# Decoder block on one core: the softmax factor moved into the transposing matrix, and eight modulation dot products moved from the a_u stage to gate B

## The chip, the core and the metric

The kernel runs on one core of a Trainium2 chip. The metric is device time in microseconds (us) of one execution, median of several. TensorE (PE) multiplies matrices, VectorE (DVE) and ScalarE (ACT) work element by element, GpSimd (POOL) takes some of that work, and SyncE (SP) issues most of the loads from HBM. Each engine executes its own instructions strictly in the order in which the program gives them; semaphores order work between engines.

## What is computed

A conditioned decoder block for 512 positions and 1024 channels. Cut to what the change touches:

```python
mod = silu(c) @ w_ada + b_ada            # shift1, scale1, gate1, shift2, scale2, gate2
h = rms_norm(x, norm1_g) * (1 + scale1) + shift1
a_u, a_v, q, k, v, qi, ki, wi, g_a, g_b = split(h @ w_in)
y_a = chunked_gmlp(gelu(a_u), gelu(a_v), ...)
# y_b: causal attention, 8 heads, over the top-k keys that the indexer selects
p = softmax(att); o = p @ v_sel
merged = sigmoid(g_a) * (y_a @ w_proj_a) + sigmoid(g_b) * (y_b @ w_proj_b)
x = x + gate1 * (merged @ w_out)         # then RMSNorm, modulation, SwiGLU FFN
```

Two details matter. The division of the softmax by its row sum can stand anywhere between the exponential and the product with V. And every entry of `mod` is a dot product of a row of the transposed `w_ada` with silu(c): gate1 (section 2 in the code), shift2 (3) and scale2 (4) take eight dot products of 128 entries each.

## The kernel before

Most products are formed from two halves of a number (`hi`, `lo`), as three matmuls of type fp32r (`mm3`, lines 66 to 68), so that a product of 128x128 weights with 512 columns is three matmuls. The program is written by hand in one order. The stages in question:

- **a_u** (159 to 222 us): `opt_b(W_AU[g], ...)` for four groups of 256 columns; between them DVE works on the gMLP and on the top-k search.
- **gate A and projection A** (222 to 291 us): two rounds of `xround` and four groups of `W_PA`.
- **attention and gate B** (291 to 373 us): 16 units `u` of two heads each, first four units over 512 keys, then four over 384, 256 and 128. The loop over `s` (line 1260) runs four steps of different units side by side: `at_pv(s-3)`, `at_qk(s)` with `at_soft_a(s)`, `at_T(s-2)`, `at_soft_b(s-1)`, the exponential `at_exp(s)`, and after these one or two K tiles of gate B (`gb_part`, list `GBN`; matmuls `pgb`). Gate B's weights are eight chunks, two for each group of `W_GB`.
- **projection B** from 373 us on.

For a unit, `at_soft_a` (L1183) adds the mask and takes row maxima on DVE, `at_exp` (L1193) exponentiates on ACT and gives row sums, `at_soft_b` takes reciprocals (L1200) and scales the two probability tiles on DVE (L1202). `at_T` (L1216) transposes them block by block with PE into PSUM (`pT`), ACT copies that to `th` (L1273), DVE forms the rest `tl` (L1274), and `at_pv` multiplies with V.

**The stream of loads.** `stream` lists the weight chunks ("w") and the modulation rows ("m") in the order of their use; `group(..., nm=, mraw=)` puts `nm` rows behind each chunk, taken from one iterator (`mm_`: sections 2, 3, 4 in this order). `get(i, ahead)` prepares everything up to two chunks ahead: for a chunk ACT makes `hi` (L134) and DVE or POOL `lo` (L138), for a row DVE does the dot product (L209: one custom instruction and one read of the accumulator). A load takes its buffer in the order of the stream. Rows of the a_u stage use the single buffer `acc`, rows of projection A the buffers A2 and A3 (`mraw`), rows of gate B (`mraw=False`) the three `raw` buffers that the weight chunks use too (`RAWB = 3`), so that a load there waits for the third load before it to be used up. SP issues them in order (L107, L115, L205).

Of the kernel before, what the change touches and what calls it, by code (L numbers as in the profile page):

```python
# [9 lines left out]
F32 = mybir.dt.float32  # L10
F32R = mybir.dt.float32r
I32 = mybir.dt.int32
AF = mybir.ActivationFunctionType
OP = mybir.AluOpType
# [14 lines left out]
def block_kernel(ctx: ExitStack, tc: tile.TileContext, x, x_t, c_row, positions, w_ada_t, w_first, w_in, w_blocks,  # L29
# [3 lines left out]
    T, V, A, P, SY = nc.tensor, nc.vector, nc.scalar, nc.gpsimd, nc.sync  # L33
    ctx.enter_context(tc.manual_schedule())
    tiny = ctx.enter_context(tc.tile_pool(name="tiny", bufs=1))
    base = ctx.enter_context(tc.tile_pool(name="base", bufs=1))
# [3 lines left out]
    w_in, w_ffn_in, w_ffn_out = w_in[0], w_ffn_in[0], w_ffn_out[0]  # L40
# [14 lines left out]
    def bank(k, name="bank"):  # L55
        return psum.tile([128, 512], F32, name=name, tag=f"b{k}", bufs=1)

    def f(ap):
        return ap.bitcast(F32)
# [22 lines left out]
    def add_w(src, kts, c0, n, lo=None, where=None):  # L82
        stream.append(dict(kind="w", src=src, kts=kts, c0=c0, n=n, lo=lo or V, where=where))
        wseq.append(len(stream) - 1)
        return len(stream) - 1

    def add_m(dma, fn, early=False, mid=True):
        stream.append(dict(kind="m", fn=fn, dma=dma, early=early, mid=not early and mid))
        return len(stream) - 1
# [76 lines left out]
    def get(i, ahead=2):  # L166
        k = wseq.index(i)
        ensure(wseq[min(k + ahead, len(wseq) - 1)])
        return chunk[i]
# [10 lines left out]
    ident = tiny.tile([128, 128], F32, name="ident")  # L180
# [50 lines left out]
    def group(src, c0, n=256, K=8, mods=None, pool=False, where=None, nm=1, mraw="A2"):  # L231
        ids = []
        for k0 in range(0, K, 4):
            ids.append(add_w(src, list(range(k0, min(K, k0 + 4))), c0, n,
                             P if pool == 2 or pool and k0 % 8 == 0 else V, where.pop(0) if where else None))
            for _ in range(nm if isinstance(nm, int) else nm[k0 // 4]):
                m = next(mods, None) if mods is not None else None
                if m is not None:
                    add_m(*m, mid=mods is mm_ and (mraw[k0 // 4] if isinstance(mraw, tuple) else mraw))
        return ids  # L240
# [12 lines left out]
    def mods_mid():  # L253
        for sec in (2, 3, 4):
            yield from mod_sec(sec)
    mm_ = mods_mid()
    dram = ctx.enter_context(tc.tile_pool(name="dram", bufs=1, space=bass.MemoryType.DRAM))
    W_AV = [[add_w(w_in, [k0, k0 + 1], 1024 + 512 * h, 512, V if k0 % 4 else P) for k0 in range(0, 8, 2)] for h in range(2)]
    W_AU = [group(w_in, 256 * g, pool=2, mods=mm_, mraw="acc") for g in range(4)]
    xsum = {(r, n): dram.tile([128, 1024], F32, name=f"xsum{r}{n}") for r in range(2) for n in (1, 2, 3, 4)}  # L260

    def blk(r, k):
# [15 lines left out]
    for r in range(2):  # L278
# [2 lines left out]
            W_X[r].append(add_w(b, [0, 1, 2, 3], 0, 256, V if p in (2, 5) else P, 48 if p in (1, 4) else 16))  # L281
        for g in (2 * r, 2 * r + 1):
            W_PA.append(group(w_pa, 256 * g, mods=mm_, pool=True, nm=(1 - g % 2,) * 2, mraw=("A2", "A3") if g % 2 == 0 else "A2"))
    W_GB = [group(w_in, 5192 + 256 * g, pool=2 * (g == 1), mods=mm_, nm=1, mraw=False)
            for g in range(4)]
    stream[W_GB[1][0]]["lo"] = V
    W_PB = [group(w_pb, 256 * g, mods=mm_, nm=((0, 1), (1, 1), (1, 0), (0, 0))[g], mraw="k_hi") for g in range(4)]
# [499 lines left out]
    def opt_b(ids, K, rhs, banks, evac, per_chunk=None, post=None, midway=None, step=None, ahead=2, t0=0):  # L787
        pb = [bank(b, "pb") for b in banks]
        for i in ids:
            if per_chunk:  # L790
                per_chunk()
            hi, lo = get(i, ahead)
            kts = stream[i]["kts"]
            for j, kt in enumerate(kts):
                for m in range(2):
                    cc = slice(m * 128, (m + 1) * 128)
                    mm3(pb[m][:, t0:], (hi[:, j, cc], lo[:, j, cc]), tuple(t[:, t0:] for t in rhs[kt]), kt == 0,
                        kt == K - 1)
                if midway and j == 1:
                    midway()  # L800
            if step:
                step()
            if i == W_PB[3][-1]:
                sec_tasks(True)
            if i == ids[-1]:
                evac(pb)
            if post:
                post()
            sec_tasks()
# [8 lines left out]
    def nbanks():  # L818
        GB_[0] ^= 1
        return (0, 1) if GB_[0] else (2, 3)  # L820
# [222 lines left out]
    def au_evac(g):  # L1043
        def ev(pb):
            u = mid.tile([128, 2, S], F32, name="u", tag="A1" if g % 2 else "A0", bufs=1)
            for m in range(2):
                A.activation(u[:, m], pb[m], AF.Gelu_apprx_tanh)
                ub[2 * g + m] = u[:, m]
        return ev

    for g in range(4):
        opt_b(W_AU[g], 8, hT, nbanks(), au_evac(g), au_tasks, au_post)


    aun = [(i, hp) for i in (3, 2, 1, 0) for hp in range(4)]
    AS = {}
# [131 lines left out]
    def at_exp(u):  # L1188
        i, hp = aun[u]
        n = (i + 1) * 128  # L1190
        pt, mx = AS["p", u]
        for e in range(2):
            A.activation(pt[e][:, :n], pt[e][:, :n], AF.Exp, scale=SCALE, bias=mx[:, 2 + e:3 + e],  # L1193
                         accum_out=mx[:, 4 + e:5 + e])

    def at_soft_b(u):
        i, hp = aun[u]
        n = (i + 1) * 128
        pt, mx = AS["p", u]
        V.reciprocal(mx[:, 6:8], mx[:, 4:6])  # L1200
        for e in range(2):
            V.tensor_scalar(pt[e][:, :n], pt[e][:, :n], mx[:, 6 + e:7 + e], None, op0=OP.mult)  # L1202

    def at_T(u):
        i, hp = aun[u]
        pt, _ = AS["p", u]
        th = mid.tile([128, 4, 2, 128], F32R, name="th", tag="A2", bufs=1)
        tl = mid.tile([128, 4, 2, 128], F32R, name="tl", tag="A3", bufs=1)
        AS["t", u] = (th, tl)
        ev = []  # L1210
        for s0 in range(0, i + 1, 2):
            ns = min(2, i + 1 - s0)
            p = bank(4 + s0 // 2, "pT")
            for s in range(ns):
                for e in range(2):
                    T.transpose(p[:, (s * 2 + e) * 128:(s * 2 + e + 1) * 128],  # L1216
                                pt[e][:, (s0 + s) * 128:(s0 + s + 1) * 128], ident)
            o = th[:, s0:s0 + ns].rearrange("p s e n -> p (s e n)")
            ol = tl[:, s0:s0 + ns].rearrange("p s e n -> p (s e n)")
            ev.append((o, ol, p[:, :ns * 256]))  # L1220
        return ev

    def at_pv(u):
        i, hp = aun[u]
        th, tl = AS["t", u]
        g = hp // 2
        p = bank(6, "pv")
        for s in range(i + 1):
            mm3(p[:, :256], (v_hi[:, s, g * 128:(g + 1) * 128], v_lo[:, s, g * 128:(g + 1) * 128]),
                (th[:, s].rearrange("p e n -> p (e n)"), tl[:, s].rearrange("p e n -> p (e n)")),  # L1230
                s == 0, s == i)
        o = slice(i * 128, (i + 1) * 128)
        pp = p[:, :256].rearrange("p (e n) -> p e n", e=2)
        return S2B[hp][:, :, o], S2B[4 + hp][:, :, o], pp

    NU = len(aun)
    gbp = {}

    def gb_part(n, ahead=2):
        for k in range(gbn[0], min(gbn[0] + n, 32)):  # L1240
            g, kt = divmod(k, 8)
            i = W_GB[g][kt // 4]
            hi, lo = get(i, ahead)
# [16 lines left out]
    for s in range(NU + 3):  # L1260
        if s >= 3:
            yh, yl, pp = at_pv(s - 3)
            A.activation(yh, pp, AF.Copy)
            V.tensor_sub(yl, pp, f(yh))
        if s < NU:
            at_qk(s)
            at_soft_a(s)
            if s == 0:
                pa_last[0]()
                at_split(2)  # L1270
        if 2 <= s <= NU + 1:
            for o, ol, p in at_T(s - 2):
                A.activation(o, p, AF.Copy)  # L1273
                V.tensor_sub(ol, p, f(o))  # L1274
        if 1 <= s <= NU:
            at_soft_b(s - 1)
        low = at_split(s + 2, True) if 0 < s < NU - 2 else lambda: None
        if s < NU:
            at_exp(s)
        low()  # L1280
        gb_part(GBN[s], 2 if s else 1)
    mbank[0] = 6
# [503 lines left out]
    for q in range(-2, NQ):  # L1786
        g, u = 2 + q // 2, q % 2
        d = sd[q]
# [210 lines left out]
    for tk in range(2):  # L1999
        for z in range(2) if tk else (None,):  # L2000
# [4 lines left out]
            n = c.stop - c.start  # L2005
# [12 lines left out]
            else:  # L2018
# [3 lines left out]
                                       scale=1.0 / 1024, scalar=ss2[:, tk, 3:4], op0=OP.mult, op1=OP.add,  # L2022
# [62 lines left out]
```

## Time and profile before

| | before |
|---|---|
| median of 3 runs | 791.38 us (791.23 to 862.42) |
| the profiled execution, its own time | 791.98 us |
| its span, first to last instruction | 790.0 us |
| PE busy | 778.3 us (99%) |
| DVE busy | 663.7 us (84%) |
| ACT busy | 443.2 us (56%) |

Busy is the union of an engine's instructions. For PE the end of a matmul is modelled and lies behind the start of the next one, so PE's rate is read from the distance between starts. The chain of waits is followed back from the last instruction; where two engines are equally late, it shows one of them.

### The profile page before, as it was taken

Reading aid. Unit: us, or ns where it says so; the run is one execution under the profiler, and the core shown is the slowest. Engines: PE = TensorE matmul, PEld = TensorE weight load, DVE = VectorE, ACT = ScalarE, POOL = GpSimd, SP = SyncE. Lnnn points to the kernel's source line nnn. Section 1 sums busy time; section 2 is a strip of 40 time slices with the busy share of each in tenths; the row PEclk is TensorE's granted clock in tenths of the full one; section 3 lists DMA queues with packets and bytes.
Section 4 is the critical chain, followed back from the end, with each engine's and each line's share of the span. In section 5 each row is a group of like instructions: output and inputs, shape, how many; then the busy total and the mean of one; then the engine's idle time right before and its main releaser. Section 6 shows DMA issues by size and latency. Waiting matters only on the chain.

```text
span 790.0 us, 12600 instructions
## 1 busy us (share of the span) xinstructions
PE 778.3 (99%) x4747; PEld 694.5 (88%) x4747; DVE 663.7 (84%) x1114; ACT 443.2 (56%) x777; POOL 181.4 (23%) x220
## 2 busy tenths in 40 slices
PE   8999999999999999999999999999999999999996
PEld 6779988878988988988888899999999999878885
DVE  5988887688897799886787879889999888898777
ACT  6556455443362636666536577555665566576654
POOL 2064234574353501000010000313121322100001
PEclk9999999999999999999999999999999999999999
DMA  9959454789763733148692503989998968666664
GB/s 361 416 156 242 119 146 122 217 231 243 212 215 107 235 112 107 54 135 278 232 234 56 187 1 107 255 251 268 258 259 222 260 201 212 177 200 209 209 192 147
DMA packets 89887, 155.05 MB, mean 196 GB/s; under 512 B 7010, under 2 KB 54770, under 8 KB 89635
## 3 DMA queue, kind: packets, MB, share of 16 engines
q1 hardware_dynamic: 72976, 116.05, 44.6%
q0 software_dynamic: 15952, 37.17, 20.9%
q10 hardware_dynamic: 898, 1.04, 0.4%
q8 instruction: 37, 0.61, 0.3%
q14 instruction: 24, 0.19, 0.1%
HBM read 150.16 MB, written 33.56 MB: 233 GB/s over the span
## 4 chain that ended last, share of the span: by engine, by line
PE 64%; DVE 17%; DMA 9%; ACT 5%; issue 4%; POOL 0%; SPq 0%; POOLq 0%; ACTq 0%; DVEq 0%
PE R L66 5%; PE R L68 5%; PE R L67 5%; PE pb L66 5%; PE pb L67 5%; PE pb L68 5%; DMA mraw<-in_w_ada_t_dram 3%; DMA raw<-in_w_ffn_in_dram 3%; DMA raw<-in_w_ffn_out_dram 3%; PE pfo L67 2%; PE pfo L68 2%; PE pfo L66 2%; PE pav L66 2%; PE pav L67 2%; PE pav L68 2%
## 5 line engine op out<-in xcount | busy, mean ns | idle before, releaser
L134 ACT ACTIVATE hi<-raw 128x1024 fp32r<-128x1024 f32 (+1 forms) x111 | 114.5, 1032 | 81.6 <-PE pb L67 32.4
L138 DVE TENSOR_TENSOR lo<-raw,hi 128x1024 fp32r<-128x1024 f32 (+2 forms) x77 | 90.3, 1174 | 26.9 <-ACT hi L134 26.0
L138 POOL TENSOR_TENSOR lo<-raw,hi 128x1024 fp32r<-128x1024 f32 x27 | 69.5, 2577 | 100.2 <-ACT hi L134 69.6
L67 PE MATMUL pfo<-lo,za 128*128 128x512 f32 (+1 forms) x144 | 55.5, 386 | 0.2 <-DVE lo L138 0.2
L66 PE MATMUL pfo<-hi,za 128*128 128x512 f32 (+1 forms) x144 | 55.5, 385 | 0.0
L68 PE MATMUL pfo<-hi,za 128*128 128x512 f32 (+1 forms) x144 | 55.3, 384 | 0.0
L209 DVE CUSTOM_DVE_ANT_0 mraw<-mraw,scb,cols 128x1024 f32<-128x1024 f32 x24 | 37.6, 1568 | 11.7 <-DMA mraw<-in_w_ada_t_dram 11.7
L66 PE MATMUL R<-tb,sx 128*128 128x256 f32 x160 | 45.0, 281 | 0.3 <-ACT gr L462 0.3
L67 PE MATMUL R<-tb,sx 128*128 128x256 f32 x160 | 44.3, 277 | 0.0
L68 PE MATMUL R<-tb,sx 128*128 128x256 f32 x160 | 44.3, 277 | 0.0
L68 PE MATMUL R<-tb,lo 128*128 128x256 f32 x160 | 44.2, 277 | 0.0
L67 PE MATMUL R<-tb,hi 128*128 128x256 f32 x160 | 44.2, 276 | 0.0
L66 PE MATMUL R<-tb,hi 128*128 128x256 f32 x160 | 44.2, 276 | 0.0
L66 PE MATMUL pb<-h,hi 128*128 128x512 f32 (+1 forms) x112 | 42.7, 382 | 0.0
L68 PE MATMUL pb<-h,lo 128*128 128x512 f32 (+1 forms) x112 | 41.9, 374 | 0.0
L67 PE MATMUL pb<-h,hi 128*128 128x512 f32 (+1 forms) x112 | 41.9, 374 | 0.0
L351 POOL COPY sm<-sm 128x1 f32<-128x1 f32 x36 | 23.2, 644 | 78.7 <-ACT sm L350 78.7
L331 POOL DMA_DIRECT2D wsum<-in_w_ffn_out_dram x24 | 21.2, 885 | 78.0 <-DMA wsum<-wsum 46.1
L66 PEld LDWEIGHTS pfo<-hi,za 128*128 128x128 f32 x144 | 27.1, 188 | 6.1 <-ACT ps L1925 0.6
L67 PEld LDWEIGHTS pfo<-lo,za 128*128 128x128 f32 x144 | 27.1, 188 | 6.1 <-DVE lo L138 0.9
L68 PEld LDWEIGHTS pfo<-hi,za 128*128 128x128 f32 x144 | 27.1, 188 | 5.2
L66 PEld LDWEIGHTS R<-tb,sx 128*128 128x128 f32 x160 | 30.1, 188 | 0.9 <-ACT gr L462 0.5
(398 smaller groups left out, 2697.0 us busy)
## 6 DMA issues: line engine op xcount, KB each, us to landing
raw<-in_w_ffn_in_dram SPq DMA_DIRECT2D x44, 512.0 KB, 5.7
raw<-in_w_in_dram SPq DMA_DIRECT2D x30, 512.0 KB, 3.8
wsum<-in_w_ffn_out_dram POOLq DMA_DIRECT2D x30, 512.0 KB, 8.3
mraw<-in_w_ada_t_dram SPq DMA_DIRECT2D x24, 512.0 KB, 6.3
raw<-wsum SPq DMA_DIRECT2D x20, 512.0 KB, 3.8
s<-in_w_ada_t_dram SPq DMA_DIRECT2D x16, 512.0 KB, 8.8
raw<-in_w_ffn_out_dram SPq DMA_DIRECT2D x16, 512.0 KB, 4.6
xsum<-in_w_blocks_dram POOLq DMA_DIRECT2D x12, 512.0 KB, 6.3
```

The lines of the kernel that those rows point to most:

```text
L66: T.matmul(o, wh, rh, start=start, stop=False, **kw)
L67: T.matmul(o, wh, rlo, start=False, stop=False, **kw)
L68: T.matmul(o, wlo, rh, start=False, stop=stop, **kw)
L134: A.activation(hi[:, :m], e["raw"][:, :m], AF.Copy)
L138: e["lo"].tensor_sub(lo[:, :m], e["raw"][:, :m], f(hi[:, :m]))
L209: V.tensor_tensor_reduce(out=raw[:, o], in0=raw[:, o], in1=c, scale=1.0, scalar=col if o.start else bias, op0=OP.mult, op1=OP.add, accum_o ...
L331: P.dma_start(wsum[n][o], src, accum_op=OP.add)
L351: P.tensor_copy(t, t)
```

## The change

`at_soft_b` no longer scales the probabilities. Instead `at_diag`, called one step after the exponential, has ACT write two 128x128 matrices per unit that hold the reciprocal row sums on their diagonal, and `at_T` multiplies by these, with an ordinary fp32 matmul in place of the transpose. The matrices live in one tile `dg` with four places, in a buffer (`hs4`) that gate A leaves free. And the a_u groups take no modulation rows any more, while gate B takes two behind each chunk in place of one; since the iterator is shared, projection A and gate B also work on other rows than before, in the same number there (four) and twice the number here (sixteen).

```diff
-    W_AU = [group(w_in, 256 * g, pool=2, mods=mm_, mraw="acc") for g in range(4)]
+    W_AU = [group(w_in, 256 * g, pool=2) for g in range(4)]
...
-    W_GB = [group(w_in, 5192 + 256 * g, pool=2 * (g == 1), mods=mm_, nm=1, mraw=False)
+    W_GB = [group(w_in, 5192 + 256 * g, pool=2 * (g == 1), mods=mm_, nm=2, mraw=False)
...
         V.reciprocal(mx[:, 6:8], mx[:, 4:6])
+
+    dgs = []
+
+    def at_diag(u):
+        if not dgs:
+            dgs.append(base.tile([128, 4, 2, 128], F32, name="dg", tag="hs4", bufs=1))
+        mx = AS["p", u][1]
+        AS["d", u] = dgs[0][:, u % 4]
         for e in range(2):
-            V.tensor_scalar(pt[e][:, :n], pt[e][:, :n], mx[:, 6 + e:7 + e], None, op0=OP.mult)
+            A.activation(AS["d", u][:, e], ident, AF.Copy, scale=mx[:, 6 + e:7 + e])
...
-                    T.transpose(p[:, (s * 2 + e) * 128:(s * 2 + e + 1) * 128],
-                                pt[e][:, (s0 + s) * 128:(s0 + s + 1) * 128], ident)
+                    T.matmul(p[:, (s * 2 + e) * 128:(s * 2 + e + 1) * 128],
+                             pt[e][:, (s0 + s) * 128:(s0 + s + 1) * 128], AS["d", u][:, e], start=True, stop=True)
...
             at_exp(s)
+        if 1 <= s <= NU:
+            at_diag(s - 1)
         low()
```

On PE, in step 2 of the attention loop (`qk` are the scores of unit 2, `pT` the turned probabilities of unit 0, `pgb` gate B):

```order
 L67 MATMUL qk<-k_lo,qh 128x512
 L68 MATMUL qk<-k_hi,ql 128x512
-L1216 MATMUL pT<-ident,pt 128x128 x8
+L1224 MATMUL pT<-dg,pt 128x128 x8
 L66 MATMUL pgb<-h_155,hi 128x512
 L67 MATMUL pgb<-h_157,hi 128x512
```

The eight instructions stand where they stood; the right-hand operand is `dg`, and so is it in the 15 other units (80 instructions in all).

On DVE, at the end of projection A, just ahead of the first unit's `at_soft_a` (L1183; `raw,GG` and `raw,Gc` are modulation dot products, the rows of 128x1 their accumulator, `lo` is gate B's second chunk):

```order
 L773 TENSOR_SCALAR sco_638<-sco_638 128x256
 L1070 TENSOR_TENSOR ql<-qf_615,qh 128x256
-L209 ISA raw,Gc<-raw,scb,cols 128x1024
-L209 ISA Gc 128x1
+L209 ISA raw,GG_88<-raw,scb,cols 128x1024
+L209 ISA GG_88 128x1
+L209 ISA raw,GG_88<-raw,scb,cols 128x1024
+L209 ISA GG_88 128x1
 L138 TENSOR_TENSOR lo<-raw,hi 128x1024
 L1183 ISA pt,mx<-qk,sco_640 128x512
```

A second dot product stands in front of the chunk's `lo` and the first unit's softmax; likewise at the seven later places where a chunk is prepared.

On SP's queue, the loads of gate B's first chunks (`raw<-in_w_in_dram`) and rows (`raw<-in_w_ada_t_dram`):

```order
 L115 DMA raw<-in_w_in_dram 128x4x256
-L205 DMA raw<-in_w_ada_t_dram 128x1024
+L205 DMA raw<-in_w_ada_t_dram 128x1024 x2
 L115 DMA raw<-in_w_in_dram 128x4x256
-L205 DMA raw<-in_w_ada_t_dram 128x1024
+L205 DMA raw<-in_w_ada_t_dram 128x1024 x2
```

With three buffers, the load of a chunk now takes the buffer of the chunk before it, where it took that of the load ahead of that chunk.

## Rows read from the trace of the kernel before

**Rows 1.** The page's header and its slices of PE and PE's clock.

```profile
span 790.0 us, 12600 instructions
PE   8999999999999999999999999999999999999996
PEclk9999999999999999999999999999999999999999
```

**Rows 2.** Waits (engine, line, waited for: us in total, times, longest), two rows.

```profile
ACT yb L1263 <- PE pv L68: 11.5, 13, 1.7
...
PE zx L1116 <- DVE zx L1126: 0.4, 1, 0.4
```

**Rows 3.** Busy time by stage: a_u, and attention with gate B.

```profile
core 0: us, PE busy (x) PEld busy (x) DVE busy (x) ACT busy (x) POOL busy (x), PEclk, DMA share, GB/s
159.00:222.00 63.00, 63.00 (x366) 54.99 (x365) 53.89 (x94) 28.13 (x37) 32.63 (x20) 1.00 0.79 216
...
291.30:372.90 81.60, 81.49 (x481) 72.08 (x480) 68.23 (x201) 52.04 (x130) 5.59 (x5) 1.00 0.45 145
```

**Rows 4.** Groups of PE by form, 291.3 to 372.9: count, busy us, mean ns, idle before.

```profile
L66 PE MATMUL pgb<-h,hi 128*128 128x512 f32 x64 | 26.5, 414 | 0.0
...
L1216 PE MATMUL pT<-ident,pt 128*128 128x128 f32 x80 | 11.3, 273 | 0.0
...
L1166 PE MATMUL qk<-k_pl,qf 128*128 128x128 f32 x16 | 2.4, 275 | 0.0
```

**Rows 5.** The chain of waits, 308.6 to 372.9, by line.

```profile
by line: PE pgb L66 18.7%; PE pgb L68 18.6%; PE pgb L67 18.5%; PE pT L1216 10.9%; PE pv L67 7.0%; PE pv L68 6.4%; PE pv L66 6.4%; PE qk L68 3.7%; PE qk L67 3.7%; PE qk L66 3.7%; PE qk L1166 2.8%
```

**Rows 6.** The chain of waits, single pieces: start, us to the next piece, what, how many.

```profile
311.16 0.87 PE pT L1216 x8
312.03 0.23 PE pgb L66
...
350.18 0.45 PE qk L1166 x4
350.62 0.44 PE pT L1216 x4
```

**Rows 7.** Groups of DVE, 290 to 375: the scaling and gate B's dot products.

```profile
L1202 DVE TENSOR_SCALAR pt<-pt,mx 128x512 f32<-128x512 f32 (+3 forms) x32 | 10.9, 384 | 0.6
L209 DVE CUSTOM_DVE_ANT_0 raw<-raw,scb,cols 128x1024 f32<-128x1024 f32 x8 | 10.2, 1280 | 0.0
```

**Rows 8.** ACT on 128x128 elements, by form, whole span.

```profile
L1193 ACT ACTIVATE pt<-pt,mx 128x128 f32<-128x128 f32 x8 | 3.2, 395 | 1.8 <-DVE mx L1185 1.8
L424 ACT ACTIVATE sn<-ropes 128x128 f32<-128x128 f32 x1 | 0.3, 296 | 0.0
```

**Rows 9.** SP's issues around gate B's first chunks; last, time to landing of `raw` loads.

```profile
283.82 0.37 SPq L115 DMA_DIRECT2D raw<-in_w_in_dram  x1
288.40 0.34 SPq L205 DMA_DIRECT2D raw<-in_w_ada_t_dram  x1
...
DMA to landing us min/median/max: 3.3/3.8/4.5
```

**Rows 10.** DVE and ACT around the first unit's softmax, in time.

```profile
287.15 1.22 DVE L138 TENSOR_TENSOR lo<-raw,hi 128x1024 fp32r<-128x1024 f32 x1
287.60 1.06 ACT L134 ACTIVATE hi<-raw 128x1024 fp32r<-128x1024 f32 x1 [5.81 <-DMA raw<-in_w_in_dram]
289.09 1.28 DVE L209 CUSTOM_DVE_ANT_0 raw<-raw,scb,cols 128x1024 f32<-128x1024 f32 x1
292.20 0.69 DVE L1183 CUSTOM_DVE_ANT_0 pt<-qk,sco 128x512 f32<-128x512 f32 x1 [0.68 <-PE qk L68]
```

**Rows 11.** The chain of waits, 303 to 309 us: start, us to the next piece, what.

```profile
303.22 0.88 DVE pt L1202 x2
...
307.92 0.60 DVE tl L1274
...
308.56 0.40 PE pv L67
```

## The prediction

> **What bounds the kernel now.** I began with the page's slices. PE's row reads 9 in all but the first and last of its 40 slices, and the row of its granted clock reads 9 in every one [rows 1]. Busy alone proves little, since the ends of matmuls are modelled. So I read the waits next: in the whole span PE waited for DVE just once for as much as 0.4 us, in the a_u stage behind VectorE's `zx` [rows 2]. The busy times by stage say the same of the two stages that the change touches: PE 63.00 of 63.00 us in a_u, 81.49 of 81.60 us in attention with gate B, where DVE has 68.2 and ACT 52.0 us [rows 3]. Last I followed the chain of waits through the attention stage. From 308.6 to 372.9 us every piece of it is a matmul: gate B 55.8%, transposes 10.9%, the rest scores and values [rows 5]. No DVE, ACT or DMA piece occurs. So here an instruction added to PE lengthens the kernel by its whole cost, and one taken from DVE shortens it by nothing. Ahead of that, from 292 to 308 us, the chain runs over DVE: the softmax, the scaling and `tl` follow each other with hardly a gap until `pv` starts at 308.56 [rows 11]. There both engines are full at once.
>
> **The products on PE.** The change turns 80 transposes [rows 4] into 80 fp32 matmuls of the same shape: 4 units times 8, 6, 4 and 2 blocks. What a transpose costs is the distance between starts, not its 273 ns: eight last 0.87 us and four 0.44 us [rows 6], 0.109 us each. The trace has no product with `dg`, but it has its twin two pieces away: the scores of the last four units, plain fp32 matmuls of 128x128 with 128 columns (L1166). The code issues two of them per unit, eight in all, and the trace has 16 records [rows 4], so one matmul is two passes; four records last 0.45 us [rows 6], which makes 0.225 us a matmul. So 80 x (0.225 - 0.109) = 9.3 us, all of it on the path. From below the change could cost nothing here if `dg` ran in one pass as the identity does; nothing in the rows says so, since the operand's type is that of L1166. From above nothing dearer is near: weight loads of this form already lie within the 0.45 us. I take 9.3 us.
>
> A rule of the Trainium skill speaks against the change more strongly. "TensorE: Matmul & The Clock Gate" (section Terms) says that the transpose mode is four times faster for FP32, and "FP8 and Floating Point Precision" (section TensorE Precision Notes) that true FP32 takes four passes through the array. By the first rule a product would cost three more transposes than a transpose does, 80 x 3 x 0.109 = 26 us. The measured ratio of the twin to the transpose is 0.225 / 0.109 = 2.1, not four, and that is what I go by.
>
> **VectorE.** Removed are 32 scalings, 10.9 us [rows 7]. Added to the stage are eight dot products; the eight that stand there take 1.280 us each, 10.2 us in all [rows 7]. So DVE's load in the stage stays as it was, and since PE's part grows by 9.3 us, DVE has more room than before from 309 us on. Both are covered by PE's matmuls and count as nothing. In the a_u stage DVE loses the eight dot products and the waits for their rows. PE was full there, so the most that this returns is the 0.4 us of [rows 2]; between 0 and 0.4 I take 0.4, because the dot products precede that `zx` on DVE.
>
> **ScalarE.** 32 writes of a diagonal block. No ACT copy of 128x128 with a per-row scale is in the trace; the nearest are a sine at 0.296 us and the exponential at 0.395 us [rows 8], so 9.5 to 12.6 us more on an engine with 52 of 81.6 us busy [rows 3]. Its place matters more: it stands right behind the next unit's exponential, and `at_T` of the following step waits for it. Behind the exponential ACT now waits for PE's `pv`, 13 times and 11.5 us in all [rows 2], and the product comes after `pv` and `qk` in PE's order, so the two writes fit into that wait. I take nothing; if that cover were gone, 0.8 us (two writes) a step would show.
>
> **The loads of gate B.** Eight rows move from SP's a_u stretch into the stage in which the DMA engines are at a share of 0.45, from one in which they were at 0.79 [rows 3]; bandwidth is no question. The buffers are. With two rows between chunks and three buffers, gate B's second chunk now takes the buffer of the first one. That is free only when DVE has made the first chunk's `lo`, which starts at 287.15 and lasts 1.22 us [rows 10]; before, the chunk was issued at 283.82, and it was the next row that was issued at 288.40 [rows 9]. So this load moves by 4.6 us to 288.4, lands 3.8 us later [rows 9] at 292.2, ACT makes `hi` in 1.06 us and DVE `lo` in 1.22 us [rows 10]: 294.45. DVE's softmax of the first unit, which started at 292.20 [rows 10], is queued behind that `lo`: 2.25 us late. What follows on DVE up to the second unit's `tl` loses two pairs of scalings (0.88 us a pair [rows 11], 1.75 us) and gains two dot products (2.56 us). So `tl`, whose first half ended at 308.5, ends it at 308.5 + 2.25 - 1.75 + 2.56 = 311.56. PE reaches the `pv` that reads it two transposed units later than 308.56, at 308.56 + 2 x 0.93 = 310.4. The stall is 1.1 us. It is bounded from below by nothing (if the load is early after all, `tl` ends at 309.3, ahead of PE) and from above by 2.25 us, the whole lateness. I take 1.1 us. Later bursts lie 8 to 12 us apart in time, and from a dot product to the landing of the third load there are 1.28 x 2 + 1.22 + 3.8 = 7.6 us, so they should find their loads landed.
>
> **The sum.** 791.98 us (the profiled execution's own time, 0.6 us above the median of the runs) + 9.3 + 1.1 - 0.4 = 802.0 us; against the median of 791.4 us that is 801.4 us, 1.3% slower.
>
> **The rivals.**
> 1. *DVE's relief pays for the products: about 791 us, not slower.* The first attention units are DVE's chain, and the scaling stood between exponential and transpose there. If PE's stream had hidden gaps of 9 us, the time would stay. For it: the DVE pieces from 292 to 308 us. Against it: a chain of nothing but matmuls for the next 64 us, and a single wait of 0.4 us [rows 2, 5]. It decides only if a product costs no more than a transpose. 4%.
> 2. *Every burst waits, not only the first: about 812 us, slower by over 2%.* Each chunk now needs three loads through three buffers in one burst of DVE. If the rows land later than the 7.6 us worked out, DVE stands still in front of the next softmax eight times; at 1.4 us a time that is 11 us beside the 9.3 us. The point from which it decides is a landing some 4 us longer than the 3.3 to 4.5 us of [rows 9]; the DMA share of 0.45 [rows 3] speaks against that. 5%.
> 3. *A product with `dg` takes as long as four transposes: 80 x 3 x 0.109 = 26 us more, 818 us.* For it stands only that no product with `dg` is in the trace; the twin's 0.225 us in the same stage [rows 6] speaks against it. 3%. The rule of the Trainium skill quoted above would have it so.
>
> **How the numbers follow.** The forecast (products at two passes, at most a small stall at the start of the stage) has 88%, and its own range is 799.5 us (9.3 us less small gains) to 804.5 us (the 2.25 us bound and 1.5 us for ACT's place). The range for 8 in 10 reaches a little to either side: 798.8 to 806.0 us. A difference of 2% is about what a measurement of this kernel can tell from no change; that is 807.2 us upwards and 775.5 us downwards. Rivals 2 and 3 give slower 8%; nothing in the profile gives 16 us back, so faster has 1%, and within 2% has 91%.
>
> **What would show it.** In the profile after: `pT` on PE with 160 records, eight matmuls lasting 1.8 us in the chain; the stage from the first `qk` to projection B about 10 us longer than 81.6; the chain still all PE from the third unit on; a wait of PE of about 1 us near the second or third step, with ACT's `hi` of gate B's second chunk starting near 292 us; no wait for `dg` above some tenths; the 0.4 us before `zx` gone. The prediction is wrong if eight products last 0.9 us or 3.5 us, if PE waits in each of the later steps with a new chunk, or if a stage outside 159 to 373 us changes by more than 1 us.

## The result and the profile after

The change makes the kernel 1.5% slower: 803.0 us (802.24 to 804.29, four runs) beside 791.6 us, a ratio of 1.0147 with a 95% interval of 1.0127 to 1.0167. One of the four runs of the kernel before, at 862.42 us, was a slow execution; the ratio leaves it out and goes by the 791.38 us of the other three. The forecast was 801.4 us, with a range of 798.8 to 806.0 us. The header and the engines' busy times, from the page of the kernel after:

```profile
span 802.3 us, 12764 instructions
...
PE 788.9 (98%) x4827; PEld 703.8 (88%) x4827; DVE 653.4 (81%) x1082; ACT 451.9 (56%) x809; POOL 182.5 (23%) x220
```

PE has about ten microseconds more, DVE ten less, and the span follows PE. The busy times of the two changed stages of the kernel after, in the columns of [rows 3]:

```profile
core 0: us, PE busy (x) PEld busy (x) DVE busy (x) ACT busy (x) POOL busy (x), PEclk, DMA share, GB/s
159.00:222.00 63.00, 63.00 (x364) 54.88 (x364) 45.28 (x81) 28.13 (x37) 32.43 (x20) 1.00 0.65 168
290.90:384.20 93.30, 91.84 (x563) 81.50 (x562) 66.71 (x183) 62.28 (x164) 4.62 (x5) 1.00 0.52 169
```

Against [rows 3], the attention stage grew from 81.6 to 93.3 us, 11.7 of the 12.3 us by which the span grew (790.0 to 802.3). PE's other work there is the same, so the difference has two parts: longer busy time, and 1.46 us in which PE had nothing to do, where it was 0.11 us before. The a_u stage lost 8.6 us of DVE's work and gained no time for it, because PE was full there already. What PE waited for in the attention stage, and the group of the products, of the kernel after:

```profile
PE qk L66 <- DVE mx L1183: 0.6, 1, 0.6
PE pv L67 <- DVE tl L1282: 0.5, 2, 0.3
PE pT L1224 <- ACT dg L1210: 0.4, 1, 0.4
```

```profile
L1224 PE MATMUL pT<-dg,pt 128*128 128x128 f32 x160 | 20.8, 277 | 0.4 <-ACT dg L1210 0.4
```

The 80 products leave 160 records, two for each, as the scores of L1166 did [rows 4]. The chain of waits through the start of the stage (start, us to the next piece, what):

```profile
286.38 1.13 DVE lo L138
287.54 3.64 DMA raw<-in_w_in_dram
291.29 1.07 ACT hi L134
...
293.52 0.68 DVE pt L1183
294.36 0.47 PE qk L66
...
300.08 1.92 PE pT L1224 x16
...
306.89 1.04 ACT hi L134
...
308.23 0.42 DVE yb L1272
...
309.91 0.52 DVE mx L1185
310.43 0.60 DVE tl L1282
311.08 0.39 PE pv L67
```

The prediction described these rows up to the softmax of the first unit: the load of gate B's second chunk (287.54) starts at the end of the first chunk's `lo`, lands in 3.64 us, and the softmax (`pt` of L1183) starts at 293.52, where it started at 292.20 before [rows 10]. What it did not have is the row behind: PE's `qk` of the second unit waits for that softmax until 294.36. Sixteen records of products last 1.92 us, later pieces 1.78 us, where eight transposes lasted 0.87 us [rows 6]. From `pv` at 311.08 on come matmuls alone, up to a second place, at the end of the stage, which the prediction did not have:

```profile
364.67 7.62 DMA raw<-in_w_proj_b_dram
...
372.31 1.07 ACT hi L134
...
373.41 1.23 DVE lo L138
...
375.62 0.88 ACT pt L1193 x4
376.50 0.30 ACT dg L1210
...
376.85 0.78 PE pT L1224 x4
```

A load took 7.62 us, twice the 3.8 us of [rows 9], and `hi`, `lo`, the softmax, the exponential and `dg` stood behind it, one after the other, until PE got its operand at 376.85.

### The profile page after: what moved, and what is told of

Read it like the earlier page. It is cut to its first block, busy times and chain, and to the rows that moved or that the text cites. A ratio compares the mean times of both kernels' runs of the same rounds, so it can differ in the third digit from the quotient of the medians.

```text
span 802.3 us, 12764 instructions
## 1 busy us (share of the span) xinstructions
PE 788.9 (98%) x4827; PEld 703.8 (88%) x4827; DVE 653.4 (81%) x1082; ACT 451.9 (56%) x809; POOL 182.5 (23%) x220
## 4 chain that ended last, share of the span: by engine, by line
PE 72%; DVE 14%; ACT 6%; DMA 5%; issue 3%; POOL 0%; SPq 0%; POOLq 0%; ACTq 0%; DVEq 0%
PE R L66 6%; PE R L67 6%; PE R L68 6%; PE pb L66 6%; PE pb L67 6%; PE pb L68 6%; PE pfo L67 4%; PE pfo L66 3%; PE pfo L68 3%; PE pT L1224 2%; PE zx L1117 2%; PE zx L1116 2%; PE zx L1119 2%; PE o L550 2%; DMA raw<-in_w_ffn_out_dram 1%
## 5 line engine op out<-in xcount | busy, mean ns | idle before, releaser
L138 POOL TENSOR_TENSOR lo<-raw,hi 128x1024 fp32r<-128x1024 f32 x27 | 67.6, 2504 | 104.3 <-ACT hi L134 104.2
L351 POOL COPY sm<-sm 128x1 f32<-128x1 f32 x36 | 25.2, 701 | 85.6 <-ACT sm L350 85.6
L66 PEld LDWEIGHTS R<-tb,sx 128*128 128x128 f32 x160 | 30.1, 188 | 1.0 <-ACT R L1830 0.5
L68 PEld LDWEIGHTS R<-tb,sx 128*128 128x128 f32 x160 | 30.1, 188 | 0.0
```

The source lines that it names most:

```text
L66: T.matmul(o, wh, rh, start=start, stop=False, **kw)
L68: T.matmul(o, wlo, rh, start=False, stop=stop, **kw)
L138: e["lo"].tensor_sub(lo[:, :m], e["raw"][:, :m], f(hi[:, :m]))
L351: P.tensor_copy(t, t)
```

## The experiments

Four explanations stood against each other: the products alone cost what the twin in [rows 6] costs; the moved dot products cost time by the buffers in which their rows land; the scalings taken from DVE were worth something after all; and ACT's writes of `dg` come late. The first runs do one part alone, the next change the buffers, the last ask why two of them missed their expectations. The stage is always the distance from the first `qk` of attention to the first matmul of projection B, read from PE's records.

### The products alone

`e1_diag_only`: the kernel after, with the stream of loads of the kernel before.

```diff
-    W_AU = [group(w_in, 256 * g, pool=2) for g in range(4)]
+    W_AU = [group(w_in, 256 * g, pool=2, mods=mm_, mraw="acc") for g in range(4)]
...
-    W_GB = [... mods=mm_, nm=2, mraw=False)
+    W_GB = [... mods=mm_, nm=1, mraw=False)
```

> The diagonal matrix and the fp32 product alone; the modulation rows stay in the a_u stage, one behind each chunk of gate B, as before. Theory A (the product's second pass on PE is the cost): 791.6 + 9.3 = 800.9 us, stage from the first score product to projection B 90.9 us, no stall of PE in its first steps, since gate B's second chunk is loaded as before. Theory B (ACT's diagonal writes make PE wait): about 1 us more than that, with waits of pT for dg. Theory C (the moved dot products cost the time): 791.6 us, no difference.

Measured: 800.93 us beside 792.14, ratio 1.0106 (1.0086 to 1.0126). The stage in this run:

```profile
291.30:381.70 90.40, 90.40 (x561) 81.33 (x560) 58.00 (x168) 61.34 (x162) 4.60 (x5) 1.00 0.41 127
```

PE works without a gap. It waits for nothing, `dg` included, although ACT has 9 us more to do. So ACT's place in the step costs nothing, and the scaling that DVE no longer does brings nothing here: DVE has 58 us of work in 90.

### The scalings alone

`e4_before_no_scale`: the kernel before without its 32 scalings, so the division by the row sums is left out.

```diff
         V.reciprocal(mx[:, 6:8], mx[:, 4:6])
-        for e in range(2):
-            V.tensor_scalar(pt[e][:, :n], pt[e][:, :n], mx[:, 6 + e:7 + e], None, op0=OP.mult)
```

> The kernel before without the 32 scalings on DVE; the softmax factor is left out of the result. Theory A: PE is full, so that 10.9 us less of DVE gives only the stall of 0.3 us at the second unit: 791.3 us. Theory F (DVE's relief is worth something by itself): 785 to 789 us.

Measured: 790.73 us, ratio 0.9984 (0.9972 to 0.9996). Its stage:

```profile
291.50:372.80 81.30, 81.30 (x482) 72.10 (x482) 57.61 (x168) 51.79 (x130) 4.66 (x5) 1.00 0.46 144
```

All 10.9 us of DVE's scalings [rows 7] are worth 0.4 us of the stage, which lasts 81.2 us from start to start. The median is 1.4 us below that of before, with an interval of 0.3 to 2.2 us, so a little more than the stage's 0.4 us cannot be excluded. DVE now does nearly the same work as in e1 (57.6 and 58.0 us), and ACT's writes cost nothing there, so the two stages differ by the products alone: 90.4 - 81.2 = 9.2 us for 80, 0.115 us each above a transpose. By the medians it is 800.9 - 790.7 = 10.2 us for the whole kernel.

### The dot products alone

`e2_move_only`: the kernel before with the two changed lines of the stream and nothing else.

```diff
-    W_AU = [group(w_in, 256 * g, pool=2, mods=mm_, mraw="acc") for g in range(4)]
+    W_AU = [group(w_in, 256 * g, pool=2) for g in range(4)]
...
-    W_GB = [... mods=mm_, nm=1, mraw=False)
+    W_GB = [... mods=mm_, nm=2, mraw=False)
```

> The eight dot products alone are moved to gate B; scaling on DVE and transposes as before. Theory A: DVE, which sets the pace of the first units, keeps the scalings, starts 1.3 us late behind the second chunk and has two more dot products before the second unit's tl: PE stalls about 3.9 us at the second unit's pv, and the a_u stage gives back 0.4 to 0.7 us: about 795 us. Theory C (the move is the cost of the whole change): 803 us. Theory D (the move is free, because DMA and DVE have room): 791 us.

Measured: 798.91 us, ratio 1.0081 (1.0061 to 1.0102): about 4 us above what I expected. The stage is 89.8 us long, 8.2 us more than before. First the busy times of three stretches of e2, then PE's largest wait and ACT's late `hi`:

```profile
290.50:380.30 89.80, 85.55 (x482) 73.50 (x481) 77.75 (x217) 52.57 (x132) 4.60 (x5) 0.98 0.55 178
300.00:310.00 10.00, 8.90 (x52) 7.30 (x50) 9.68 (x22) 5.32 (x12) 1.00 (x1) 1.00 0.60 188
310.00:320.00 10.00, 8.10 (x46) 7.58 (x46) 8.14 (x23) 5.20 (x15) 1.38 (x1) 0.83 0.38 129
```

```profile
PE pv L67 <- DVE tl L1274: 3.5, 3, 1.9
```

```profile
307.86 1.06 ACT L134 ACTIVATE hi<-raw 128x1024 fp32r<-128x1024 f32 x1 [2.25 <-DMA raw<-in_w_in_dram]
```

Scaling and two dot products a burst together fill DVE in 300 to 310 us (9.68 of 10). It falls behind, the buffers come free later, the third chunk's load lands at 307.8 us, and PE stalls four times (0.9, 1.3, 2.1 and 0.7 us by the distance between starts). The 0.83 of the clock in 310 to 320 us is a mean: behind the longest stall, which ends at 312.05, the granted clock was 0.50, the level of 1.2 GHz, for some 3 us, and 1.00 again from 317 us on:

```profile
314.00:316.00 2.00, 2.00 (x9) 1.90 (x8) 1.27 (x4) 0.19 (x1) 0.00 (x0) 0.50 0.81 284
```

Forecasting only the waits, I had neither the lagging DVE nor the clock. The two parts alone cost 8.8 us (e1) and 8.2 us (e2) of the stage, but together, in the kernel after, 11.7 us. So the dropped scalings and the slower PE take away 5 us of the dot products' cost in these executions: DVE's relief pays for part of the load that the same change brings, and for next to nothing else. By the medians it is 8.8 + 6.8 - 11.4, about 4 us.

### The kernel after, turned by the identity

`e3_turn_by_ident`: `dg` is still written, but the blocks are transposed as before, so the softmax factor is left out.

```diff
-                    T.matmul(p[:, ...], pt[e][:, ...], AS["d", u][:, e], start=True, stop=True)
+                    T.transpose(p[:, ...], pt[e][:, ...], ident)
```

> The changed kernel, with ACT still writing the diagonal matrices but PE turning by the identity in transposes as before; the softmax factor is left out of the result, nothing takes its place. Theory A: 80 x 0.116 = 9.3 us less than the changed kernel, given back in part, because PE comes to the second unit's pv 1.9 us earlier and meets the same late tl: 803.0 - 9.3 + 1.6 = 795.3 us. Theory E (a product costs no more than a transpose, and the waits around it are the loss): 802 us.

Measured: 795.45 us, ratio 1.0037 (1.0024 to 1.0049). Its stage:

```profile
290.70:375.60 84.90, 82.39 (x482) 71.95 (x481) 66.28 (x185) 61.50 (x164) 4.61 (x5) 1.00 0.56 181
```

Without the products 84.9 us remain, 3.3 us above the 81.6 of [rows 3]. 2.5 us of the stage are idle time of PE, at the start and at the end as in the kernel after, and once more at 304.3 us. From here to the kernel after is 93.3 - 84.9 = 8.4 us, a little less than the products' 9.2 us; with them PE is idle for 1.46 us instead of 2.5. Set beside e2, which still scales, it is the relief of DVE once more: 89.8 - 84.9 = 4.9 us of the stage, 798.9 - 795.5 = 3.5 us of the median. Part of the 4.9 us is e2's clock: some 3 us at half the rate cost about 1.5 us as an estimate, and in e3 the clock stayed at 1.00 (row above).

### A buffer of its own for the first row

`e6_row_in_acc`: the kernel after, but the first row behind each of gate B's chunks lands in the buffer `acc`, so that a chunk's load takes the buffer of the load ahead of the last chunk again.

```diff
-            for _ in range(...):
+            for j_ in range(...):
...
-                    add_m(*m, mid=mods is mm_ and (...))
+                    add_m(*m, mid=mods is mm_ and (("acc", False)[j_] if mraw == "alt" else ...))
...
-    W_GB = [... mods=mm_, nm=2, mraw=False)
+    W_GB = [... mods=mm_, nm=2, mraw="alt")
```

> The changed kernel, with the first of the two modulation rows behind each chunk of gate B loaded into the buffer acc, free in this stage, so that the weight chunks have the three raw buffers nearly as before. Theory A2 (what the stage loses beyond the products comes from chunks whose load waits for a buffer): the stalls of 0.7 us at the second unit's scores and of 1.0 us in the last units go, stage 93.3 - 2 = 91.3 us, whole 801.2 us. Theory B2 (the extra dot products on DVE and ACT's diagonal writes cause them): stage and time as in the changed kernel, 93.3 and 803.0 us.

Measured: 800.71 us beside 791.64, ratio 1.0113 (1.0093 to 1.0134). Its stage, and SP's issue of the second chunk, which stood at 287.54 in the kernel after:

```profile
290.80:381.40 90.60, 90.60 (x563) 81.53 (x563) 66.79 (x185) 61.23 (x163) 5.26 (x5) 1.00 0.51 168
```

```profile
283.24 0.38 SPq L115 DMA_DIRECT2D raw<-in_w_in_dram  x1
```

PE waits for nothing in the stage any more, at the end of it neither, and the stage is 90.5 us from first to last start, as in e1. The same dot products stand in the same places on DVE; what changed is when their loads may start. Lining up the gate-B matmuls of the two kernels one by one shows where the kernel after loses the 2.7 us: 1.48 us up to 315 us and 1.25 us near 377 us. So the buffers decide both, the wait for `dg` at 376.85 included. The median gives a similar sum: e6 lies 9.1 us above the kernel before, the kernel after 11.4 us.

### The same buffer without the relief

`e7_move_in_acc`: e2 with the rows placed by the edit of e6, so against the kernel before:

```diff
-    W_AU = [group(w_in, 256 * g, pool=2, mods=mm_, mraw="acc") for g in range(4)]
+    W_AU = [group(w_in, 256 * g, pool=2) for g in range(4)]
...
-    W_GB = [... mods=mm_, nm=1, mraw=False)
+    W_GB = [... mods=mm_, nm=2, mraw="alt")
```

> The move of the eight dot products alone (scaling on DVE and transposes as before), with the first row behind each chunk in the buffer acc. Theory A2: the stalls for late chunks go, but DVE still has two more dot products before the second unit's tl: 308.5 + 2.6 = 311.1 against PE at 308.3, some 2.8 us stay: 791.6 + 3 - 0.7 = 794 us, against 798.9 us for the move with raw buffers. Theory B2 (DVE's dot products are all of it): 798.9 us again.

Measured: 797.32 us, ratio 1.0072 (1.0051 to 1.0092), between the two expectations. PE's stall of 1.9 us at 308.4 has a cause of its own. Two rows of e7, on DVE the second dot product of the third chunk's burst, on POOL the chunk's `lo`:

```profile
306.61 3.40 DVE L209 CUSTOM_DVE_ANT_0 raw<-raw,scb,cols 128x1024 f32<-128x1024 f32 x1
```

```profile
306.43 2.49 POOL L138 TENSOR_TENSOR lo<-raw,hi 128x1024 fp32r<-128x1024 f32 x1 [32.94 <-ACT hi L134]
```

A dot product that lasts 1.28 us elsewhere took 3.40 us, and for 2.3 us of them POOL's `lo` ran beside it. That could be chance: its row might have been late. Experiment e10 below decides it. A second stall, of 1.8 us up to 312.42, follows, and here too the granted clock then falls:

```profile
314.00:316.00 2.00, 2.00 (x8) 1.90 (x7) 1.28 (x4) 0.38 (x1) 0.00 (x0) 0.50 0.04 10
```

### Half of the scalings on ACT

`e8_half_scale_on_act`: the kernel before, but the second scaling of each unit is done by ACT behind the next exponential.

```diff
-        for e in range(2):
-            V.tensor_scalar(pt[e][:, :n], pt[e][:, :n], mx[:, 6 + e:7 + e], None, op0=OP.mult)
+        V.tensor_scalar(pt[0][:, :n], pt[0][:, :n], mx[:, 6:7], None, op0=OP.mult)
...
+        A.activation(pt[1][:, :n], pt[1][:, :n], AF.Copy, scale=mx[:, 7:8])   # behind at_exp
```

> The kernel before with the second of each unit's two scalings made by ACT behind the next exponential, where the changed kernel writes its diagonal; transposes and rows as before. Frees 5.4 us of DVE at no cost to PE. Theory A: PE is full, the stall of 0.3 us at the second unit goes, 791.2 us, no difference that a measurement can tell. Theory F (DVE's relief is worth something once it costs PE nothing): 788 us or less. If ACT's longer queue makes PE wait: 793 us or more.

Measured: 792.04 us, ratio 1.0004 (0.9992 to 1.0016), no difference. DVE has 63.7 us of work in the stage instead of 68.2, and PE waits no less (idle for 0.31 us of the stage, 0.11 us before).

`e9_half_scale_move_acc`: this edit and that of e7 together.

```diff
-        for e in range(2):
-            V.tensor_scalar(pt[e][:, :n], pt[e][:, :n], mx[:, 6 + e:7 + e], None, op0=OP.mult)
+        V.tensor_scalar(pt[0][:, :n], pt[0][:, :n], mx[:, 6:7], None, op0=OP.mult)
...
-    W_GB = [... mods=mm_, nm=1, mraw=False)
+    W_GB = [... mods=mm_, nm=2, mraw="alt")
```

> Half of the scaling on ACT, the eight dot products moved to gate B with the first row behind each chunk in acc, transposes as before: the aim of the change without the product. Theory A: DVE has 0.9 us less scaling and 2.6 us more dot products before the second unit's tl, about 1.7 us of stall stay there, the a_u stage gives back 0.7 us: 792.5 us. Theory F: 789 us, below both kernels.

Measured: 796.73 us, ratio 1.0059 (1.0038 to 1.0081), 4 us above the expectation. In its trace the dot product lasts 3.43 us beside POOL's `lo`, PE stalls for 1.5 and 1.8 us between 307 and 311 us, and then, by stretch:

```profile
310.00:312.00 2.00, 0.85 (x4) 0.85 (x5) 1.93 (x7) 1.46 (x5) 0.00 (x0) 0.58 0.97 342
312.00:314.00 2.00, 2.00 (x11) 2.00 (x11) 0.62 (x2) 0.77 (x3) 0.00 (x0) 0.50 0.14 53
...
318.00:320.00 2.00, 2.00 (x16) 1.83 (x15) 1.64 (x5) 2.00 (x7) 0.00 (x0) 1.00 0.00 0
```

The granted clock (the column behind POOL's) falls to 0.50, the level of 1.2 GHz, and is back at 2.4 GHz at 318 us.

### POOL's share of the work moved to DVE

`e10_move_acc_lo_on_dve` is e7, and `e11_half_scale_acc_lo_on_dve` is e9, each with the one `lo` that POOL makes in this stage given to DVE.

```diff
-    W_GB = [group(w_in, 5192 + 256 * g, pool=2 * (g == 1), mods=mm_, nm=2, mraw="alt")
+    W_GB = [group(w_in, 5192 + 256 * g, pool=0, mods=mm_, nm=2, mraw="alt")
```

> The kernel before with the moved dot products and the first row of each burst in acc (as in the run e7), but the one lo of gate B's third chunk that POOL makes there is made by DVE, behind the two dot products. In e7 the second dot product lasted 3.40 us instead of 1.28, and POOL's lo ran from 306.43 to 308.92 beside it. Theory P (the dot product stands still while POOL's lo runs): without it every dot product lasts 1.28 us, DVE needs 1.28 + 1.22 = 2.50 us where it needed 3.40, PE's stalls near 308 us shrink by 0.9 us, the median falls from 797.3 to about 796.4, and further if PE's granted clock then stays at 1.00. Rival D (the dot product waited for its row): it still ends some 3.4 us after its start, the lo comes on top, 1.2 us more: 798.5.

> The same edit on the run e9 (half of the scalings on ACT, moved dot products, first row in acc): there the second dot product lasted 3.43 us from 305.31, POOL's lo ran from 305.27 to 307.66, PE stalled 1.5 and 1.8 us and its granted clock was 0.50 from 312 to 316. Theory P: dot product 1.28 us, the first stall 1.5 - 0.9 = 0.6 us; from 796.7 to 795.8 if the clock falls all the same, and to about 793 if it stays at 1.00 (some 3 us of PE's work were lost at half the rate). Rival D: 798 or more.

Measured: 795.87 us beside 792.38 for e10 (ratio 1.0043, 1.0028 to 1.0058), 796.5 us for e11 (1.0053, 1.0034 to 1.0071). The same dot product in e10, the `lo` behind it, and the stretch of its stage in which e9's clock had fallen:

```profile
306.07 1.28 DVE L209 CUSTOM_DVE_ANT_0 raw<-raw,scb,cols 128x1024 f32<-128x1024 f32 x1
...
307.28 1.22 DVE L138 TENSOR_TENSOR lo<-raw,hi 128x1024 fp32r<-128x1024 f32 x1
```

```profile
310.00:312.00 2.00, 1.10 (x9) 1.10 (x10) 1.93 (x8) 1.52 (x4) 0.00 (x0) 1.00 0.95 328
```

Every dot product of the stage lasts 1.27 to 1.29 us in both runs. The row was there; the dot product had stood still beside POOL. PE's stall behind it shrinks from 1.87 to 0.86 us in e10 and from 1.5 to 0.5 us in e11, and the clock stays at 1.00. In e10 the median follows (the excess over before falls from 5.7 to 3.5 us, expected 0.9 us or more). Not all of that is the dot product's: a stall near 303 us, ahead of POOL's `lo`, is shorter by 0.6 us too, and e10 lacks e7's stretch at half the clock. In e11 it hardly does: 4.1 us against 5.1, within the intervals, and short of the 3.7 us less that I allowed if the clock stayed up. The profiled execution of e9 was the slowest of its seven (799.85 us; they spread from 793.6), so its fall of the clock is that of one execution and no measure of the median. The profiled execution of e7 was the slowest of its four (798.86 us) as well. How often the clock falls in either stays open.

## Why the prediction held, and where it did not

The time came out 1.6 us above the forecast (803.0 and 801.4 us), and the profiled execution 2.3 us above its own (804.29 and 802.0 us). Of these 2.3 us, 1.25 us are a wait for a load that the prediction expected to have landed, and 1.05 us lie behind the changed stages.

**Products, 9.3 us: right.** 9.2 us from the stages of e1 and e4. The twin in [rows 6] was the right price: sixteen records of the products last 1.78 to 1.92 us, 0.111 to 0.120 us each, two for a product. "TensorE: Matmul & The Clock Gate" in the Trainium skill (section Terms) gives the transpose mode a factor of four for FP32. By that the stage would have grown by 26 us; the runs give (0.109 + 0.115) / 0.109 = 2.1.

**DVE counted as nothing: right in sum, for a reason that was only half said.** Dropping the scalings alone gives 0.4 us of the stage (e4), so rival 1 falls. But e3 against e2 shows that without the dropped scalings the dot products would have cost 4.9 us more of the stage (3.5 us of the median). The prediction had it as load exchanged for load; it did not see how close DVE is to being the bound between 300 and 310 us if only one of the two edits is made.

**ACT counted as nothing: right.** 32 writes of 388 ns each, between the 296 and 395 ns of [rows 8]. In e1 and e6 PE never waits for `dg`. The one wait in the kernel after, 0.37 us at 376.85, is the late load passed on.

**The a_u stage, 0.4 us back: about right.** PE's wait before `zx` is gone. The distance from the first `zx` of gate A to projection A's first matmul went from 21.8 to 21.2 us, and projection A lost another 0.2.

**The start of the stage, 1.1 us: right in sum, but in two pieces and not in one.** The load starts at 287.54 (forecast 288.4), the first unit's softmax at 293.52 (294.45), and `tl` ends its first half at 311.03 (311.56). The prediction put the whole loss at the `pv` that reads this `tl`. Lined up against e6, PE loses 0.84 us of its 1.48 us already at 294.36, where the second unit's `qk` waits for the first unit's softmax, a wait that the prediction did not have, and 0.46 us at `pv`. The kernel before, lined up against e4, loses 0.37 us at this `pv`, so 1.1 us remain. The sum could hold because the end of `tl` sets it, and the earlier wait only takes part of it beforehand; that is read from the rows and not tested by a run. One part of the wait was in the trace of before without my naming it: `mx` of L1185 lasts 0.52 us at 309.91 (0.69 us in the kernel before) instead of 0.17, until POOL's `lo` ends.

**Later bursts find their loads landed: this step failed**, at one of seven places. The prediction has "from a dot product to the landing of the third load there are 1.28 x 2 + 1.22 + 3.8 = 7.6 us", with the 3.8 us of [rows 9] for a landing, and "bandwidth is no question". For the six bursts inside gate B the wait stayed away. The last chunk prepared in the stage is projection B's first one, and there the landing was 7.62 us by itself. SP's issues (the row of three begins with this load; the others follow at 371.02 and 372.23) and POOL's in the kernel after, and the busy times of 366 to 373 us:

```profile
364.67 7.93 SPq L115 DMA_DIRECT2D raw<-in_w_proj_b_dram  x3
```

```profile
363.84 0.54 POOL L1298 DMA_DIRECT2D xr<-in_x_dram  x1 [4.18 <-PE qk L1166]
368.72 0.53 POOL L1298 DMA_DIRECT2D xr<-in_x_dram  x1 [4.34 <-PE pT L1224]
```

```profile
366.00:373.00 7.00, 7.00 (x45) 6.25 (x44) 4.06 (x14) 4.87 (x17) 0.87 (x2) 1.00 0.88 296
```

POOL loads the rows of the residual at this time, from its own queue, and the DMA engines are at 0.88 where I had taken the stage's mean of 0.45 [rows 3]. POOL's loads alone do not make the landing long, for all twelve traces have them. In the four that leave the rows in the a_u stage (before, e1, e4, e8) projection B's first load lands in 3.4 to 3.5 us, in the eight that move them in 6.6 to 7.6 us. Its landing in the kernel before and in e6:

```profile
DMA to landing us min/median/max: 3.5/3.5/3.5
DMA to landing us min/median/max: 7.1/7.1/7.1
```

In the eight, SP issues a row at most 1.2 us ahead of this load (in the kernel after two rows, at 362.32 and 363.53, with POOL's load at 363.84 and this one at 364.67); in the four it issues none for the 7.6 us ahead of it. So the moved rows are among the transfers that the prediction called no question. POOL's load lies closer to it in the eight too; how much is the rows' part and how much POOL's no run separates. In e6 the load lands as slowly, but it is issued at 361.99, 7.3 us ahead of its `hi`, and nobody waits. In the kernel before, projection B's first load was issued 12.6 us ahead of its `hi`, so a slow landing cost nothing; in the one after it has to wait for the buffer of gate B's last chunk and comes 7.6 us ahead. ACT's `hi` then waits 1.41 us for it, and PE loses 1.25 us. I had looked at SP's queue and at the mean of the kernel before, not at what the moved rows and the other queue would load together at the end of the stage. Rival 2 had this mechanism at every burst; it occurred at two of eight. Rival 3 falls with the price of a product.

**The rest.** 9.2 + 1.5 + 1.25 is 11.9 us; less the 0.4 us by which the stage of before exceeds that of e4, 11.5 of its 11.7 us. Behind the stage the span grows by another 1.05 us, mostly in the tail of the FFN, where PE waits 0.7 us for DVE's `lo` at three places. No part of the change lies there. The twelve traces take 415.9 to 418.2 us from projection B's first matmul to the end, and two kernels that are the same there, before (417.1) and e4 (415.9), lie 1.2 us apart; so 1.05 us is no more than single executions differ. The prediction had named a change of more than 1 us outside the two stages as a sign of being wrong; by this spread, one trace on either side cannot tell.

## What to carry to other kernels

Work put on the engine that already filled every slice cost its whole price here, and a twin of the new instruction in the same trace gave that price better than a rule did. Work taken from another engine was worth next to nothing by itself; it was worth 3.5 to 5 us, but only against the load that the same edit put there. When rows and chunks share a ring of buffers, follow each load to the instruction that frees its buffer, and look at every queue that is loading at that moment, with what the change itself adds, not at the stage's mean.

## What was not expected of the hardware

- **A DVE dot product and POOL's `lo` exclude each other.** 3.40 and 3.43 us beside POOL (e7, e9), 1.28 us without it (e10, e11), where DVE makes that `lo` itself, behind the dot product. It goes the other way too: in the kernel before and in e6, gate B's third burst has a dot product of 1.28 us, and it is POOL's `lo` beside it that takes 3.38 and 3.05 us, where the median of its 27 is 2.42. The two rows of before:

```profile
304.35 1.28 DVE L209 CUSTOM_DVE_ANT_0 raw<-raw,scb,cols 128x1024 f32<-128x1024 f32 x1
304.51 3.38 POOL L138 TENSOR_TENSOR lo<-raw,hi 128x1024 fp32r<-128x1024 f32 x1 [30.61 <-DVE ql L1069]
```

Here the dot product started first and kept its time; in e7 POOL's `lo` did (306.43 and 306.61). That does not settle which of the two gives way, for in a_u of the kernel before it is the dot product again, although it starts 0.6 us ahead. Its dot product there, and the first of two `lo` beside it:

```profile
159.24 4.53 DVE L209 CUSTOM_DVE_ANT_0 mraw<-mraw,scb,cols 128x1024 f32<-128x1024 f32 x1
```

```profile
159.85 2.83 POOL L138 TENSOR_TENSOR lo<-raw,hi 128x1024 fp32r<-128x1024 f32 x1
```

The Trainium skill's "GPSIMD Engine Reference" (section 1. Specifications) says that GpSimd shares its SBUF interfaces with VectorE and contends with DVE instructions that read two SBUF inputs or run in a 2-port performance mode. The trace agrees for the first kind: the dot product reads a row (`raw` or `mraw`) and `scb`, while the softmax step of L1183, which reads scores from PSUM, lasts its 0.68 us beside POOL's `lo` as without it.

- **A stall of PE can cost more than itself.** In e9's profiled execution PE stood still for 3.3 us in two pieces, the second up to 311.15; the granted clock was 0.58 in 310 to 312 us and 0.50 from 312 to 316 us, with matmuls of 256 columns starting 0.21 us apart instead of 0.12. Two rows of PE in e9 at either level:

```profile
311.96 0.41 PE L67 MATMUL pv<-tl,v_hi 128*128 128x256 f32 x1
312.17 0.41 PE L68 MATMUL pv<-th,v_lo 128*128 128x256 f32 x1
...
318.85 0.28 PE L67 MATMUL pv<-tl,v_hi 128*128 128x256 f32 x1
318.96 0.28 PE L68 MATMUL pv<-th,v_lo 128*128 128x256 f32 x1
```

It fell to 0.50 in the profiled executions of e2 and e7 too, behind stalls of 2.1 us, and of 1.9 and 1.8 us. In the kernel after, whose stalls were each below 1 us, and in e10 and e11, with stalls of 0.9 and 1.8 and of 0.5 and 1.8 us, it stayed at 1.00. That the stalls bring the fall is read from the order in time over these traces; no run changes a stall and nothing else.
